# Reordering the start and the end of a seven-product up-projection in three chained transformer blocks

## The chip, the cores and the metric

The kernel runs on one core of a Trainium2 chip. The metric is device time in microseconds (us) of one execution, as the median of several runs. One execution was also recorded by the hardware profiler; the rows below come from it.

## The reference

The input is one sequence of 1024 tokens with 1024 features. Three blocks follow one another: the first mixes by retention and a gated unit, the second by convolution and neighbourhood attention, the third by stick-breaking and sliding-window attention. The change concerns the feed-forward parts of blocks 1 and 3, with D_FF = 2816:

```python
# block 1
h = rmsnorm(x, ffn_norm_g[l])
up = causal_depthwise_conv(h @ w_up[l], conv_w[l], conv_b[l])
a, bgate = jnp.split(up, [D_FF], axis=-1)
x = x + (jax.nn.silu(a) * bgate) @ w_down[l]
# block 3
gate, up = jnp.split(h @ w_gate_up, 2, axis=-1)
ffn = (jax.nn.silu(gate) * up) @ w_down
h = layer_norm_3(ALPHA * h + ffn, ln2_g[l], ln2_b[l])
```

## The kernel before

Activations lie with features on the 128 partitions and tokens along the free axis, in two halves of 512 tokens. Each fp32 product is made of three matmuls on split operands, `hi` (a copy in the matmul type, on ACT) and `lo` (the remainder `src - hi`, on DVE or POOL; `split`): hi·hi, lo·hi and hi·lo.

An up-projection has 22 chunks of 128 gate and 128 up features. The first `lead` chunks (3 in block 1, 2 in block 3) are plain products, two by `first_quad` (tile `fq`, 4 weight tiles `whi`/`wlo` in each token half) and, in block 1, chunk 2 by `gemm_a`. While `first_quad` computes, the normalization of the second half is still being made (tiles `rs_s`, `r`, `row`, `hhi`). The other chunks go through `strassen` (L1258): the 2 x 2 block product of (gate, up) weights and (feature, token) halves of the input, by seven products of 12 matmuls each, summed in three PSUM banks `p1`, `p2`, `p3`. Per group (one chunk, index `n`) the weights need sums and splits, in six steps `s0` to `s5` (`s_steps`, L1204): A22 (`shi`/`slo`); two sums on POOL (`raw<-raw`); S1 and S3 (`shi`/`slo`); A1 (`whi`/`wlo`); two more sums; S24 (`whi`/`wlo`). Steps of group n+1 are issued between the products of group n. The weights come in pairs of tiles `raw` by `s_dma`, from the buffer pools `wp` and `up` in turn. The input side needs T1 to T4, made once per block in `gen_t` (L1176): differences of `X` in place on DVE, then `thi` on ACT and `tlo`.

Of the sums, `e1` (copy of the first bank, on ACT) and `v1`, `v2` (bank plus `e1`, on DVE) lead to outputs; S3·T3 overwrites the bank that `v1` reads, A22·T4 the bank that `v2` reads. The outputs of a chunk go through convolution and silu (block 1: copy `u` by `put`, then `conv`: `carry`, `t`, `a`, `g`) or gating (block 3); `later(c)` returns this work as closures, which run during the next group. `g` goes to DRAM (`gd`) and comes back as `gx` for the down-projection.

The down-projection `down` (tile `dn`) takes the chunks in pairs: for each of 16 outputs six matmuls and one addition to `X`. Its preparation is `tail(0)` to `tail(3)`, issued between the products of the last group: weights, loads of `gx` and `X`, and the splits `ghi`/`glo`.

Nothing reorders the program: each engine runs its instructions in the order in which the code issues them, and waits at the first that is not ready. Banks of PSUM (6, tag `b`), `h` buffers (64) and the tiles `whi`, `wlo` (4 each) set how far one engine may run ahead.

Of the kernel before, what the change touches and what calls it, by code (L numbers as in the profile page):

```python
# [12 lines left out]
ALU = mybir.AluOpType  # L13
# [82 lines left out]

S_TILES = ((38, 76), (178, 218))

_VEC = [
    ("mix_norm_g", 8), ("ret_norm_g", 4), ("ffn_norm_g", 8), ("conv_b", 44), ("final_norm_g", 8),
# [196 lines left out]
class Kernel:  # L299
    def __init__(self, tc, ins, outs, blocks=(1, 2, 3)):  # L300
        self.tc, self.nc, self.a, self.o = tc, tc.nc, ins, outs
        self.blocks = blocks
        self.drv = Driver()
        self.wn = 0
        self.wl, self.raws = [], []
        self.wi = self.wd = 0
        self.stops = [lo for lo, _ in S_TILES]


    def h(self, name="h", dt=F32, shape=(128, HF), tag="h"):  # L310
# [45 lines left out]


    def w_dma(self):
        if self.wd < self.a["wall"].shape[0]:
            raw = self.wp.tile([128, 1024], F32, tag="raw", bufs=2, name="raw")  # L360
            self.nc.sync.dma_start(out=raw, in_=self.a["wall"][self.wd])
            self.wd += 1
            self.raws.append(raw)

    def w_more(self):
        return self.wi < (self.stops[0] if self.stops else self.a["wall"].shape[0])

    def w_load(self):

        if not self.w_more():  # L370
            return
        nc = self.nc
        while len(self.raws) < min(2, self.a["wall"].shape[0] - self.wi):
# [170 lines left out]
            self.drv.drain()  # L544


    def first_quad(self, evac, hook=None):

        ws = self.w_take(4)
        for half in range(2):
            self.drv.force(self.hs[half])
            pend = []
            for g in (0, 2):
                pss = [self.bank("fq") for _ in range(2)]
                if half == 1 and hook:
                    hook()
                yield from self.gemm_q(pss, ws[g:g + 2], half, middle=hook if half == 1 and g else None)
                pend += [(g + i, half, ps) for i, ps in enumerate(pss)]  # L560
                if half == 1:
# [614 lines left out]
    def gen_t(self):  # L1176

        X, T = self.X, self.T  # L1180
        V, P = self.nc.vector, self.nc.gpsimd

        def make(i, parts):

            low = None
            for k, (x, p, q) in enumerate(parts):
                hi, lo = T[i][0][k], T[i][1][k] = self.h("thi", F32R), self.h("tlo", F32R)
                self.tt(x, p, q, ALU.subtract)
                self.act(hi, x, AF.Copy)
                if low:  # L1190
                    self.tt(*low, ALU.subtract, V)
                low = lo, x, hi
            self.tt(*low, ALU.subtract, P)

        make(1, [(X[k][0], X[k][1], X[k][0]) for k in range(4)])
        yield
        make(2, [(X[k][0], X[k + 4][1], X[k][0]) for k in range(4)])
        yield
        make(3, [(X[k][1], X[k + 4][1], X[k][1]) for k in range(4)])
        yield  # L1200
        make(4, [(X[k + 4][0], X[k + 4][0], X[k][0]) for k in range(4)])
        yield

    def s_steps(self, n, st):  # L1204
# [16 lines left out]

        def s0():
            nonlocal ra, rb
            ra, rb = self.raws[0:2]
            self.raws = self.raws[2:]
            self.wi += 2
            st["A22"] = quarter(rb[:, R])

        def s1():
# [18 lines left out]

    def s_dma(self, n):

        pool = self.up if n % 2 else self.wp
        for _ in range(2):
            raw = pool.tile([128, 1024], F32, tag="raw", bufs=2, name="raw")
            self.nc.sync.dma_start(out=raw, in_=self.a["wall"][self.wd])
            self.wd += 1
            self.raws.append(raw)

    def strassen(self, lead, put, later, rest, tail):  # L1258

        hhi, hlo = self.H
        B11, B21, B22 = (([hhi[k + o][x] for k in range(4)], [hlo[k + o][x] for k in range(4)])
                         for o, x in ((0, 0), (4, 0), (4, 1)))
# [10 lines left out]
                    yield 6 * 216.0  # L1275

        n_all = NFF - lead
        left = ([], [], [])
        cur = self.s_first
        for n in range(n_all):  # L1280
            c = n + lead
            nxt, steps = {}, []
            b1, b2, b3 = (self.bank(x) for x in ("p1", "p2", "p3"))
            if n + 2 < n_all:
                self.s_dma(n + 2)
# [3 lines left out]
                steps[1]()  # L1289
            else:  # L1290
                tail(0)
                steps = [None] * 2 + [lambda: tail(1), lambda: None, lambda: tail(2), lambda: tail(3)]
            if n == 0:
                yield from prod(b1, cur["A1"], 0, B11, True)
                steps[2]()
                yield from prod(b3, cur["S1"], 0, T[1], True)
                yield from prod(b2, cur["S24"], 0, T[2], True)
            else:
                yield from prod(b2, cur["S24"], 0, T[2], True)
                steps[2]()  # L1300
                yield from prod(b1, cur["A1"], 0, B11, True)
            e1, v1 = self.h("e1"), self.h("v1")
            self.act(e1, b1, AF.Copy)
            self.tt(v1, b2, e1, ALU.add)
# [2 lines left out]
            steps[3]()  # L1307
            for f in left[0]:
                f()
            if n > 0:  # L1310
                yield from prod(b3, cur["S1"], 0, T[1], True)
            steps[4]()
            yield from prod(b2, cur["S3"], 0, T[3], False)
            v2 = self.h("v2")
            self.tt(v2, b2, e1, ALU.add)
            put(c, 1, 1, b3, v2)
            steps[5]()
            yield from prod(b1, cur["A1"], 512, B21, False)
# [8 lines left out]
            put(c, 0, 1, b3, v1)  # L1327
            left = later(c)
            cur = nxt
        for part in left:  # L1330
            for f in part:
                f()

    def ffn(self, evac, put, later, add_last, done, by_half, alpha=None, lead=2):

# [4 lines left out]
        with ExitStack() as ctx:  # L1340
            self.up = ctx.enter_context(self.tc.tile_pool(name="ffn", bufs=4))
            self.pt = ctx.enter_context(self.tc.tile_pool(name="ffnp", bufs=2, space=PSUM))
            self.T = {i: ([None] * 4, [None] * 4) for i in range(1, 5)}
            self.s_first = {}
            steps = self.s_steps(0, self.s_first)
            gt = self.gen_t()

            def step(n):
                for _ in range(n):
                    steps.pop(0)()  # L1350

            def hook():

                next(gt)
                if lead == 2:
                    step(2)
                    if len(steps) == 4:
# [6 lines left out]
            def g_split(c, half, own):  # L1364
# [3 lines left out]
                self.split(hi, lo, x, eng=nc.vector if half else None)  # L1368
                G[c, half] = hi, lo

            def g_group(i):
# [8 lines left out]
            def tail(n):  # L1380

                if n == 0:
                    del self.stops[0]
                    self.w_load()
                    self.w_load()
                elif n == 1:
                    for a in g_group(0):
                        g_dma(*a[:2])
                    for j in range(2):
                        x_load(j)  # L1390
                elif n == 2:
                    for a in g_group(0):
                        g_split(*a)
                else:
                    for j in range(2, 8):
                        x_load(j)
                    for a in g_group(1):
                        g_dma(*a[:2])

            yield from self.first_quad(lambda i, half, ps: evac(i // 2, i % 2, half, ps), hook)  # L1400
            for i in range(4, 2 * lead):
                w, = self.w_take(1)
                step(3)
                if i == 5:
                    self.s_dma(1)
                    next(gt)
# [6 lines left out]
            yield from self.strassen(lead, put, later, (lambda: next(gt)) if lead == 2 else (lambda: None), tail)  # L1413

            def down(i, ws):
                n = 0
# [2 lines left out]
                for j in range(8):  # L1419
                    for half in range(2):  # L1420
# [1034 lines left out]
```

## Time and profile before

| | us |
|---|---|
| median of 3 runs | 3191.98 |
| the runs | 3191.98, 3200.32, 3191.89 |
| the profiled execution | 3198.7 |
| its span | 3196.9 |
| PE busy | 2966.0 |

The span is what the trace shows from the first instruction to the last; 1.8 us of the profiled execution lie around it. Times in the rows are counted from the span's start. PE is TensorE's matmuls, PEld its weight loads, DVE VectorE, ACT ScalarE, POOL GpSimd, SP the engine that issues the DMAs. A number in brackets is the engine's idle time ahead of the instruction, with what ended it.

### The profile page before, as it was taken

Reading aid. Unit: us, or ns where it says so; the run is one execution under the profiler, and the core shown is the slowest. Engines: PE = TensorE matmul, PEld = TensorE weight load, DVE = VectorE, ACT = ScalarE, POOL = GpSimd, SP = SyncE. Lnnn points to the kernel's source line nnn. Section 1 sums busy time; section 2 is a strip of 40 time slices with the busy share of each in tenths; the row PEclk is TensorE's granted clock in tenths of the full one; section 3 lists DMA queues with packets and bytes.
Section 4 is the critical chain, followed back from the end, with each engine's and each line's share of the span. In section 5 each row is a group of like instructions: output and inputs, shape, how many; then the busy total and the mean of one; then the engine's idle time right before and its main releaser. Section 6 shows DMA issues by size and latency. Waiting matters only on the chain. (4 is left out here: it accounts for less than half of the span.)

```text
span 3196.9 us, 41418 instructions
## 1 busy us (share of the span) xinstructions
PE 2966.0 (93%) x15188; PEld 2512.3 (79%) x15188; DVE 1813.0 (57%) x3518; ACT 1287.2 (40%) x2493; POOL 1432.2 (45%) x1012
## 2 busy tenths in 40 slices
PE   8999996999989999889998989988799899999997
PEld 6898785888868878768897778877678688887886
DVE  6443255566665568976655664666767522224556
ACT  4232234444431243556673356644434422222223
POOL 4313424777733364863214352143333577674330
PEclk9999998999999999999998999989889999999997
DMA  4101231222243212131113232100212222225321
GB/s 156 34 21 54 73 115 52 77 80 80 79 158 106 94 52 86 37 96 58 46 38 116 92 121 63 45 19 22 67 66 96 83 79 80 88 74 175 102 83 53
DMA packets 114876, 248.96 MB, mean 78 GB/s; under 512 B 19696, under 2 KB 31600, under 8 KB 114672
## 3 DMA queue, kind: packets, MB, share of 16 engines
q1 hardware_dynamic: 114384, 246.01, 23.6%
q8 instruction: 120, 1.97, 0.3%
q14 instruction: 84, 0.69, 0.1%
q10 hardware_dynamic: 288, 0.30, 0.0%
HBM read 192.52 MB, written 53.74 MB: 77 GB/s over the span
## 5 line engine op out<-in xcount | busy, mean ns | idle before, releaser
L331 POOL TENSOR_TENSOR wlo<-raw,whi 128x1024 fp32r<-128x1024 f32 x240 | 581.4, 2432 | 868.2 <-ACT whi L325 827.4
L325 ACT ACTIVATE whi<-raw 128x1024 fp32r<-128x1024 f32 x240 | 248.0, 1053 | 566.8 <-PE dn L346 315.0
L331 DVE TENSOR_TENSOR X<-dn,X 128x512 f32<-128x512 f32 (+1 forms) x312 | 210.6, 677 | 173.4 <-PE dn L346 170.8
L346 PE MATMUL dn<-ghi,whi 128*128 128x512 f32 (+1 forms) x736 | 283.4, 385 | 5.9 <-DVE X L331 5.9
L346 PE MATMUL dn<-glo,whi 128*128 128x512 f32 (+1 forms) x736 | 282.6, 384 | 0.0
L346 PE MATMUL dn<-ghi,wlo 128*128 128x512 f32 (+1 forms) x736 | 282.3, 383 | 0.0
L346 PE MATMUL p<-thi,shi 128*128 128x512 f32 x468 | 187.8, 401 | 23.6 <-DVE v L331 22.8
L331 POOL TENSOR_TENSOR raw<-raw 128x512 f32<-128x512 f32 x156 | 201.9, 1295 | 12.1
L346 PE MATMUL p<-hhi,whi 128*128 128x512 f32 x468 | 184.5, 394 | 19.8 <-ACT whi L325 19.8
L331 DVE TENSOR_TENSOR v<-p,e 128x512 f32<-128x512 f32 x78 | 53.8, 690 | 247.8 <-ACT e L325 194.9
L346 PE MATMUL p<-hhi,wlo 128*128 128x512 f32 x468 | 184.3, 394 | 6.3 <-POOL wlo L331 6.3
L346 PE MATMUL p<-tlo,shi 128*128 128x512 f32 x468 | 186.1, 398 | 0.0
L331 POOL TENSOR_TENSOR slo<-raw,shi 128x512 fp32r<-128x512 f32 x117 | 150.7, 1302 | 78.6 <-ACT shi L325 78.6
L346 PE MATMUL p<-thi,slo 128*128 128x512 f32 x468 | 185.6, 397 | 0.0
L346 PE MATMUL p<-hlo,whi 128*128 128x512 f32 x468 | 183.4, 392 | 0.0
L328 DVE SCALAR_TENSOR_TENSOR t<-u,vec,t 128x512 f32<-128x512 f32 x176 | 133.0, 756 | 79.5 <-ACT t L325 74.1
L346 PE MATMUL qk<-hhi,whi 128*128 128x512 f32 x384 | 164.2, 428 | 8.0 <-ACT hhi L325 7.2
L331 POOL TENSOR_TENSOR beta<-beta,f 128x511 f32<-128x511 f32 (+3 forms) x96 | 89.3, 934 | 176.5 <-DVE beta L335 165.4
L346 PEld LDWEIGHTS dn<-ghi,whi 128*128 128x128 f32 x736 | 140.0, 190 | 34.1 <-DVE X L331 6.3
L346 PEld LDWEIGHTS dn<-glo,whi 128*128 128x128 f32 x736 | 140.1, 190 | 27.6
L346 PEld LDWEIGHTS dn<-ghi,wlo 128*128 128x128 f32 x736 | 140.0, 190 | 27.4
L346 PE MATMUL op<-hhi,wlo 128*128 128x512 f32 x384 | 153.5, 400 | 4.0 <-POOL wlo L331 4.0
(401 smaller groups left out, 8177.2 us busy)
## 6 DMA issues: line engine op xcount, KB each, us to landing
raw<-in_wall SPq DMA_DIRECT2D x240, 512.0 KB, 3.7
gd<-g SPq DMA_DIRECT2D x88, 256.0 KB, 2.1
gx<-gd SPq DMA_DIRECT2D x88, 256.0 KB, 4.9
x2d<-X SPq DMA_DIRECT2D x64, 256.0 KB, 2.0
X<-x2d SPq DMA_DIRECT2D x64, 256.0 KB, 5.4
x<-in_xT SPq DMA_DIRECT2D x16, 256.0 KB, 6.1
X<-in_xT SPq DMA_DIRECT2D x16, 256.0 KB, 4.4
T<-in_rpbx SPq DMA_DIRECT2D x8, 448.0 KB, 3.9
```

Source lines behind the costliest of these rows:

```text
L325: self.nc.scalar.activation(out=out, in_=in_, func=func, bias=bias, scale=scale, **kw)
L328: self.nc.vector.scalar_tensor_tensor(out=out, in0=in0, scalar=s, in1=in1, op0=op0, op1=op1)
L331: (eng or self.nc.vector).tensor_tensor(out=out, in0=in0, in1=in1, op=op)
L346: self.nc.tensor.matmul(out=out, lhsT=lhsT, rhs=rhs, start=start, stop=stop, skip_group_check=more)
```

## The change

The change alters the order of instructions, and for some the engine; the products, sums and loads are the same in number.

1. The first group's weights have a list of their own (`sraws`). In block 1 its pair of `raw` tiles is loaded at the start of `first_quad`, and s0 to s2 are issued in its first half (`hook` 1 to 3); s3 to s5 stand ahead of chunk 2. In block 3, s0 to s2 are issued in the first half, s3 to s5 in the second.
2. The input sums are made in the order T1, T3, T2, T4, all `tlo` on DVE; before, the fourth of each was on POOL.
3. The first group computes A1·B11, S24·T2, S1·T1; before, S1·T1 came second.
4. Chunk 2 of block 1 computes its second token half first, only copies its outputs (`put`), and leaves the convolutions to the first group (`later(2)`).
5. In the last group the loads of `gx` are issued behind the second product, and the splits of the first down-projection group behind `v2` and the first output, all four `glo` on POOL; before, they stood ahead of `v2`, two of them on DVE.
6. What is left of the last chunk is dealt out over the outputs of `down`; before, it stood ahead of them.

```diff
-S_TILES = ((38, 76), (178, 218))
+S_TILES = ((38, 38), (178, 180))
...
     def w_dma(self):
-        if self.wd < self.a["wall"].shape[0]:
+        if self.wd < self.stops[0][1]:
...
     def w_more(self):
-        return self.wi < (self.stops[0] if self.stops else self.a["wall"].shape[0])
+        return self.wi < self.stops[0][0]
...
     def first_quad(self, evac, hook=lambda n: None):
...
             for g in (0, 2):
                 pss = [self.bank("fq") for _ in range(2)]
-                if half == 1 and hook:
-                    hook()
-                yield from self.gemm_q(pss, ws[g:g + 2], half, middle=hook if half == 1 and g else None)
+                hook(4 * half + g)
+                yield from self.gemm_q(pss, ws[g:g + 2], half, middle=lambda: hook(4 * half + g + 1))
...
     def gen_t(self):
...
                 if low:
-                    self.tt(*low, ALU.subtract, V)
+                    self.tt(*low, ALU.subtract)
                 low = lo, x, hi
-            self.tt(*low, ALU.subtract, P)
+            self.tt(*low, ALU.subtract)
 
         make(1, [(X[k][0], X[k][1], X[k][0]) for k in range(4)])
         yield
+        make(3, [(X[k][1], X[k + 4][1], X[k][1]) for k in range(4)])
+        yield
         make(2, [(X[k][0], X[k + 4][1], X[k][0]) for k in range(4)])
-        yield
-        make(3, [(X[k][1], X[k + 4][1], X[k][1]) for k in range(4)])
         yield
         make(4, [(X[k + 4][0], X[k + 4][0], X[k][0]) for k in range(4)])
...
     def s_dma(self, n):
-        pool = self.up if n % 2 else self.wp
+        pool = self.up if (n + self.lead) % 2 else self.wp
...
     def strassen(self, put, left, later, rest, tail):
...
-        left = ([], [], [])
...
-                steps = [None] * 2 + [lambda: tail(1), lambda: None, lambda: tail(2), lambda: tail(3)]
-            if n == 0:
-                yield from prod(b1, cur["A1"], 0, B11, True)
-                steps[2]()
-                yield from prod(b3, cur["S1"], 0, T[1], True)
-                yield from prod(b2, cur["S24"], 0, T[2], True)
-            else:
+            if n > 0:
                 yield from prod(b2, cur["S24"], 0, T[2], True)
                 steps[2]()
-                yield from prod(b1, cur["A1"], 0, B11, True)
+            yield from prod(b1, cur["A1"], 0, B11, True)
+            if n == 0:
+                steps[2]()
+                yield from prod(b2, cur["S24"], 0, T[2], True)
+            if n + 1 == n_all:
+                tail(1)
...
-            if n > 0:
-                yield from prod(b3, cur["S1"], 0, T[1], True)
+            yield from prod(b3, cur["S1"], 0, T[1], True)
             steps[4]()
             yield from prod(b2, cur["S3"], 0, T[3], False)
             v2 = self.h("v2")
             self.tt(v2, b2, e1, ALU.add)
             put(c, 1, 1, b3, v2)
             steps[5]()
+            if n + 1 == n_all:
+                tail(2)
             yield from prod(b1, cur["A1"], 512, B21, False)
             put(c, 0, 0, b1, None)
             for f in left[1]:
                 f()
+            if n + 1 == n_all:
+                tail(3)
             yield from prod(b2, cur["A22"], 0, T[4], False)
...
-        for part in left:
-            for f in part:
-                f()
+        self.left = [f for part in left for f in part]
...
             def hook(n):
 
+                if n == 0 and lead == 3:
+                    self.s_dma(0)
+                elif n in (1, 2, 3):
                     steps.pop(0)()
+                elif n in (4, 6):
+                    next(gt)
+                    if n == 6 and lead == 2:
+                        for f in steps:
+                            f()
                         self.s_dma(1)
+                elif n == 7 and lead == 2:
+                    next(gt)
...
             def tail(n):
...
                 elif n == 2:
+                    for j in range(2, 5):
+                        x_load(j)
+                else:
                     for a in g_group(0):
-                        g_split(*a)
-                else:
-                    for j in range(2, 8):
+                        g_split(*a, nc.gpsimd)
+                    for j in range(5, 8):
                         x_load(j)
                     for a in g_group(1):
                         g_dma(*a[:2])
...
-            for i in range(4, 2 * lead):
-                w, = self.w_take(1)
-                step(3)
-                if i == 5:
-                    self.s_dma(1)
-                    next(gt)
-                for half in range(2):
-                    ps = self.bank("fq")
-                    yield from self.gemm_a(ps, w, half)
+            left = ([], [], [])
+            if lead == 3:
+                ws = self.w_take(2)
+                for f in steps:
+                    f()
+                self.s_dma(1)
+                for half in (1, 0):
+                    for w in range(2):
+                        ps = self.bank("fq")
+                        yield from self.gemm_a(ps, ws[w], half)
+                        put(2, w, half, ps, None)
                     if half:
-                        self.w_retire(1)
-                    evac(i // 2, i % 2, half, ps)
+                        next(gt)
+                        next(gt)
+                self.w_retire(2)
+                left = later(2)
...
             def down(i, ws):
...
                         n += 1
+                        if n % 3 == 1 and self.left:
+                            self.left.pop(0)()
                         if n % gap == 0 and loads and n > 2:
                             g_split(*loads.pop(0))
```

Three places in the instruction order. First, ACT at the end of the plain products of block 1 and in the first group of seven products (`u`, `t`, `a` are convolution work, `e` the copy `e1`). Before:

```order
149 L325 ACTIVATE u<-fq 128x512
150 L325 ACTIVATE t<-u,vec 128x512
151 L325 ACTIVATE shi<-raw 128x512 x3
152 L325 ACTIVATE u<-fq 128x512
153 L325 ACTIVATE t<-u,vec 128x512
154 L325 ACTIVATE a<-t 128x512
155 L325 ACTIVATE u<-fq 128x512
156 L325 ACTIVATE t<-u,vec 128x512
157 L325 ACTIVATE a<-t 128x512
158 L325 ACTIVATE whi<-raw 128x1024 x2
```

Now:

```order
152 L326 ACTIVATE u<-fq 128x512
153 L326 ACTIVATE t<-u,vec 128x512
154 L326 ACTIVATE whi<-raw 128x1024 x2
155 L326 ACTIVATE u<-fq 128x512 x2
156 L326 ACTIVATE thi<-X 128x512 x8
157 L326 ACTIVATE u<-fq 128x512 x2
158 L326 ACTIVATE shi<-raw 128x512 x3
159 L326 ACTIVATE e_4396<-p_4351 128x512
160 L326 ACTIVATE whi<-raw 128x1024
161 L326 ACTIVATE t<-u,vec 128x512
162 L326 ACTIVATE a<-t 128x512
163 L326 ACTIVATE t<-u,vec 128x512
```

The two `whi` copies (A1 and S24) move ahead of the convolutions of chunk 2; the three `shi` still stand ahead of `e`, and `thi` of T2 and T4 come behind `whi`.

Second, ACT in the first half of the plain products of block 1, ahead of the normalization of the second token half, where `rs_s` is the root that the rows `r` are made of. Before:

```order
122 L325 ACTIVATE whi<-raw 128x1024
123 L325 ACTIVATE sq<-X 128x512
124 L325 ACTIVATE rs_s<-ms 128x4
125 L325 ACTIVATE hhi<-X 128x512 x2
126 L325 ACTIVATE u<-fq 128x512
127 L325 ACTIVATE t<-u,vec 128x512
```

Now:

```order
122 L326 ACTIVATE whi<-raw 128x1024
123 L326 ACTIVATE sq<-X 128x512
124 L326 ACTIVATE shi<-raw 128x512
125 L326 ACTIVATE rs_s<-ms 128x4
126 L326 ACTIVATE hhi<-X 128x512 x2
127 L326 ACTIVATE u<-fq 128x512
128 L326 ACTIVATE t<-u,vec 128x512
```

One `shi`, of A22, stands ahead of `rs_s`.

Third, DVE in the last group of block 1. Before:

```order
707 L1109 COPY u<-carry 128x2
708 L328 SCALAR_TENSOR_TENSOR t<-u,vec,t 128x512 x2
709 L331 TENSOR_TENSOR glo<-gx,ghi 128x512 x2
710 L331 TENSOR_TENSOR v_7400<-p_7282,e_7340 128x512
711 L331 TENSOR_TENSOR u<-p_7283,v_7400 128x512
```

Now:

```order
707 L1109 COPY u<-carry 128x2
708 L329 SCALAR_TENSOR_TENSOR t<-u,vec,t 128x512 x2
709 L332 TENSOR_TENSOR v_7384<-p_7282,e_7340 128x512
710 L332 TENSOR_TENSOR u<-p_7283,v_7384 128x512
711 L1105 MEMSET u 128x2
712 L1107 COPY carry<-u 128x2
```

The two `glo` are gone from the row ahead of the second sum `v`.

## Rows read from the trace of the kernel before

**Rows 1.** Page, section 1: busy time, share of the span and instructions of each engine.

```profile
PE 2966.0 (93%) x15188; PEld 2512.3 (79%) x15188; DVE 1813.0 (57%) x3518; ACT 1287.2 (40%) x2493; POOL 1432.2 (45%) x1012
```

**Rows 2.** Waits of PE, whole span: us in total, times, longest us.

```profile
PE p L346 <- DVE v L331: 22.8, 4, 8.7
PE p L346 <- ACT whi L325: 21.0, 3, 16.9
...
PE p L346 <- POOL wlo L331: 9.7, 4, 5.1
...
PE dn L346 <- DVE X L331: 5.9, 1, 5.9
```

**Rows 3.** Windows: us, busy time (instructions) of each engine, granted clock of PE, DMA share, GB/s.

```profile
557.47:575.00 17.53, 17.53 (x65) 14.21 (x66) 2.77 (x4) 3.55 (x6) 14.15 (x10) 0.84 0.36 112
575.00:900.00 325.00, 325.00 (x1414) 265.68 (x1414) 203.89 (x355) 148.25 (x218) 227.96 (x148) 1.00 0.22 76
921.14:928.45 7.31, 7.30 (x24) 5.87 (x25) 5.33 (x11) 0.78 (x1) 0.00 (x0) 0.75 1.05 387
942.69:960.00 17.31, 17.31 (x64) 14.04 (x65) 10.82 (x17) 1.41 (x2) 2.00 (x3) 0.83 0.40 136
...
2909.97:2917.80 7.83, 7.83 (x25) 6.24 (x25) 2.07 (x3) 0.00 (x0) 0.00 (x0) 0.69 1.05 396
```

**Rows 4.** Timeline, all engines, 455 to 465: start us, us, engine, line, operation, tiles [idle before].

```profile
460.21 0.20 ACT L325 ACTIVATE rs_s<-ms 128x4 f32<-128x4 f32 x1 [2.87 <-DVE ms L335]
...
461.26 0.16 DVE L331 TENSOR_TENSOR r<-rs_s,rs_t 128x4 f32<-128x4 f32 x1
...
464.27 0.60 PE L454 MATMUL row<-ident,r 128*128 128x128 f32 x4
```

**Rows 5.** Page, section 6: DMA issues, KB each, median us from issue to landing.

```profile
raw<-in_wall SPq DMA_DIRECT2D x240, 512.0 KB, 3.7
```

**Rows 6.** Page, section 5: groups of POOL and ACT instructions, busy us, mean ns of one, idle before.

```profile
L331 POOL TENSOR_TENSOR wlo<-raw,whi 128x1024 fp32r<-128x1024 f32 x240 | 581.4, 2432 | 868.2 <-ACT whi L325 827.4
L325 ACT ACTIVATE whi<-raw 128x1024 fp32r<-128x1024 f32 x240 | 248.0, 1053 | 566.8 <-PE dn L346 315.0
...
L331 POOL TENSOR_TENSOR raw<-raw 128x512 f32<-128x512 f32 x156 | 201.9, 1295 | 12.1
```

**Rows 7.** Timeline, all engines, 536 to 558.

```profile
536.59 0.79 PE L346 MATMUL p<-hhi,whi 128*128 128x512 f32 x1 [16.93 <-ACT whi L325]
...
542.85 2.41 POOL L331 TENSOR_TENSOR wlo<-raw,whi 128x1024 fp32r<-128x1024 f32 x1 [1.17 <-ACT whi L325]
...
543.33 2.48 DVE L331 TENSOR_TENSOR tlo<-X,thi 128x512 fp32r<-128x512 f32 x1 [7.23 <-ACT thi L325]
...
550.84 0.61 ACT L325 ACTIVATE shi<-raw 128x512 fp32r<-128x512 f32 x1
...
557.47 0.79 PE L346 MATMUL p<-thi,shi 128*128 128x512 f32 x1 [8.71 <-DVE v L331]
```

**Rows 8.** Timeline, all engines, 918 to 922.

```profile
918.67 1.26 POOL L331 TENSOR_TENSOR glo<-gx,ghi 128x512 fp32r<-128x512 f32 x1 [0.68 <-ACT ghi L325]
...
920.41 0.68 DVE L331 TENSOR_TENSOR v<-p,e 128x512 f32<-128x512 f32 x1
...
921.14 0.79 PE L346 MATMUL p<-thi,shi 128*128 128x512 f32 x1 [6.47 <-DVE v L331]
```

**Rows 9.** Waits of PE, window 2440 to 2562.

```profile
PE p L346 <- POOL wlo L331: 8.5, 3, 5.1
PE p L346 <- ACT whi L325: 4.1, 2, 2.8
PE p L346 <- DVE v L331: 2.0, 1, 2.0
```

**Rows 10.** Timeline, all engines, 2906 to 2910.

```profile
2906.61 1.30 ACT L325 ACTIVATE ghi<-gx 128x512 fp32r<-128x512 f32 x2 [0.25 <-DMA gx<-gd]
...
2909.97 0.80 PE L346 MATMUL p<-thi,shi 128*128 128x512 f32 x1 [5.59 <-DVE v L331]
```

More of the change, by code (lines that the diff above doesn't have):

```diff
@@ L304, in __init__ @@
         self.wn = 0
-        self.wl, self.raws = [], []
+        self.wl, self.raws, self.sraws = [], [], []
         self.wi = self.wd = 0
-        self.stops = [lo for lo, _ in S_TILES]
+        n = self.a["wall"].shape[0]
+        self.stops = [*S_TILES, (n, n)]
     def h(self, name="h", dt=F32, shape=(128, HF), tag="h"):
@@ L372, in w_load @@
         nc = self.nc
-        while len(self.raws) < min(2, self.a["wall"].shape[0] - self.wi):
+        while len(self.raws) < min(2, self.stops[0][1] - self.wi):
             self.w_dma()
@@ L544, in build, with first_quad @@
             self.drv.drain()
-    def first_quad(self, evac, hook=None):
+    def first_quad(self, evac, hook=lambda n: None):
         ws = self.w_take(4)
@@ L1180, in gen_t @@
         X, T = self.X, self.T
-        V, P = self.nc.vector, self.nc.gpsimd
         def make(i, parts):
@@ L1223, in s0 @@
             nonlocal ra, rb
-            ra, rb = self.raws[0:2]
-            self.raws = self.raws[2:]
-            self.wi += 2
+            raws = self.sraws or self.raws
+            ra, rb = raws.pop(0), raws.pop(0)
             st["A22"] = quarter(rb[:, R])
@@ L1255, in s_dma, with strassen @@
             self.wd += 1
-            self.raws.append(raw)
-    def strassen(self, lead, put, later, rest, tail):
+            self.sraws.append(raw)
+    def strassen(self, put, left, later, rest, tail):
+        lead = self.lead
         hhi, hlo = self.H
@@ L1281, in strassen @@
             c = n + lead
-            nxt, steps = {}, []
+            nxt, steps = {}, [lambda: None] * 6
             b1, b2, b3 = (self.bank(x) for x in ("p1", "p2", "p3"))
@@ L1343, in ffn, with hook @@
             self.T = {i: ([None] * 4, [None] * 4) for i in range(1, 5)}
-            self.s_first = {}
+            self.s_first, self.lead = {}, lead
             steps = self.s_steps(0, self.s_first)
             gt = self.gen_t()
-            def step(n):
-                for _ in range(n):
+            def hook(n):
+                if n == 0 and lead == 3:
+                    self.s_dma(0)
+                elif n in (1, 2, 3):
                     steps.pop(0)()
-            def hook():
-                next(gt)
-                if lead == 2:
-                    step(2)
-                    if len(steps) == 4:
+                elif n in (4, 6):
[3 more added lines that the diff above has]
+                            f()
                         self.s_dma(1)
+                elif n == 7 and lead == 2:
+                    next(gt)
             def g_dma(c, half):
@@ L1362, in g_dma, with g_split @@
                 nc.sync.dma_start(out=G[c, half], in_=self.gd[c][:, HF * half:HF * half + HF])
-            def g_split(c, half, own):
+            def g_split(c, half, own, eng=None):
                 x = G[c, half]
@@ L1367, in g_split @@
                           for y in ("ghi", "glo"))
-                self.split(hi, lo, x, eng=nc.vector if half else None)
+                self.split(hi, lo, x, eng=eng or (nc.vector if half else None))
                 G[c, half] = hi, lo
@@ L1383, in tail @@
                     del self.stops[0]
+                    self.wi += 2 * (NFF - lead)
                     self.w_load()
@@ L1400, in ffn @@
             yield from self.first_quad(lambda i, half, ps: evac(i // 2, i % 2, half, ps), hook)
-            for i in range(4, 2 * lead):
-                w, = self.w_take(1)
-                step(3)
-                if i == 5:
-                    self.s_dma(1)
-                    next(gt)
-                for half in range(2):
-                    ps = self.bank("fq")
-                    yield from self.gemm_a(ps, w, half)
-                    if half:
-                        self.w_retire(1)
-                    evac(i // 2, i % 2, half, ps)
-            yield from self.strassen(lead, put, later, (lambda: next(gt)) if lead == 2 else (lambda: None), tail)
+            left = ([], [], [])
[9 more added lines that the diff above has]
+                        put(2, w, half, ps, None)
+                    if half:
+                        next(gt)
+                        next(gt)
+                self.w_retire(2)
+                left = later(2)
+            yield from self.strassen(put, left, later, (lambda: next(gt)) if lead == 2 else (lambda: None), tail)
             def down(i, ws):
```

## The prediction

> **What bounds the kernel now.** I read the page first: TensorE (PE) is busy for 2966.0 of 3196.9 us [rows 1], so time can only come out of the 231 us in which it idles, and out of stretches in which it runs slowly. Next I read the list of what PE waited for over the whole program [rows 2], where the reader should look at tile names: waits of `p`, the seven-product scheme, are 22.8 us on the sum `v`, 21.0 on the weight copy `whi` and 9.7 on the weight remainder `wlo`; `dn`, the down-projection, has one wait of 5.9 on `X`. The change touches only tiles of these kinds. A timeline of PE then shows where they lie: at the first group and behind the last group of products in blocks 1 and 3. I call the four places A (start, block 1), B (end, block 1), C (start, block 3) and D (end, block 3).
>
> A wait costs more than its length. In the steady part of block 1, 1414 matmuls take 325.0 us at granted clock 1.00, which is 0.230 us each. Behind the wait that ends at 557.47, 65 take 17.53 us at 0.84, instead of 14.9; behind 921.14, 24 take 7.30 instead of 5.5; behind 942.69, 64 take 17.31 instead of 14.7; behind 2909.97, 25 take 7.83 instead of 5.8 [rows 3]. So 1.8 to 2.6 us come on top of each longer wait. Granted clocks of 0.69 to 0.84 over a window are mixtures of the two levels, 2.4 and 1.2 GHz.
>
> **Place A.** Chunk 2's plain products end at 519.66 (536.59 less 16.93), and the fourth seven-product matmul group, S3·T3, starts at 557.47 [rows 7]. That is 37.8 us for 36 matmuls, which at 0.230 are worth 8.3; 29.5 us are lost. Two waits make most of it: 16.93, because ACT does the convolutions of chunk 2 ahead of `whi`, and 8.71, because ACT does three `shi` that wait for sums on POOL ahead of the copy `e` that `v` needs.
>
> Now the same stretch with the new order. The first pair of weights is loaded early, and its first `shi` stands on ACT ahead of `rs_s`, the root for the normalization. In the trace `rs_s` ran at 460.21, its result `r` was there at 461.42, and PE used it at 464.27 [rows 4]. A weight tile lands 3.7 us after its issue in the median [rows 5]; two tiles behind the copies that SP issues there I put at 465.8. Then `shi` ends at 466.4, `r` is ready 1.2 later, at 467.6, and PE stands still 3.4 us. Another 0.5 goes to the remainders of chunk 2, whose place on POOL moves back. Chunk 2 ends at 519.66 + 3.9 = 523.6.
>
> Because chunk 2's convolutions are now left for the next group, ACT copies A1's `whi` before that end; I put its end at 518.4. POOL follows with `wlo` (2.43), two sums (1.30 each) and, after one `whi` copy of 1.05, the next `wlo` [rows 6]: 520.9, 523.5, 524.6, 527.0. A1·B11 waits for nothing. S24·T2 needs the last `wlo` and four T2 remainders on DVE, which alternate with differences behind the POOL instruction: 530.3. S24·T2 ends near 531, S1·T1 near 533.7. Behind T4's four copies ACT starts the three `shi` of the next group at about 536.0, and from the first `shi` to S3·T3 it took 6.63 before (550.84 to 557.47 [rows 7]) with the same instructions in between. So S3·T3 starts at 542.6, 14.9 us sooner. Bounds: if the early tiles land at once, 18; if they land 7 us later than I think, 8. The 8.7 wait is not cured, it stays at 8.9: `e` still stands behind `shi`. **14.9.**
>
> **Place B.** PE waits 6.47 for `v` at 921.14; DVE did that sum at 920.41, behind two remainders `glo`, which wait for `gx` from memory [rows 8]. With all four `glo` on POOL and behind the second sum, `v` follows the last convolution directly, and I put its end at 916.1; as PE was free at 914.67, 1.5 of the wait is left. Gain 5.0, and 1.8 of slow matmuls behind it. Four `glo` at 1.26 on POOL [rows 8] end at about 923.2 if the first starts at 918.0; the down-projection, now due at 921.6, needs its third then, and the fourth for its second output. That just fits. The 5.9 us on `X` [rows 2] came because all left-over convolutions stood ahead of the first `X` on DVE; dealt out over the down-projection they fit into the six banks that PE may fill ahead, worth some 8 us, of which I see 2.6 used. Gain 5.9, and 2.6 behind it. Bounds: 5 to 18. **15.3.**
>
> **Place C.** Waits of 8.5, 4.1 and 2.0 in the window [rows 9]. Weights come earlier (two steps in the first half) and T1, T3 are formed before T2, so that S1·T1 and S3·T3 are ready when wanted. What is late next is T2: its copies stand behind the `whi` of S24, which I put at 2512.4, and its last remainder at 2518.0. By the same chain as in A, S3·T3 starts at 2524.5, which is 6.0 before its place in the trace; I take 5.5, since PE will again be slow behind the 4.8 us wait that is left. Bounds: 0 to 11. **5.5.**
>
> **Place D.** PE waits 5.59 at 2909.97 for `v` behind `glo` again, and the last two of the copies `ghi` that they follow come at 2906.61 to 2907.91 [rows 10]. Now `v` is ready before PE is, about 0.3 of the wait stays, and 2.1 of slow matmuls goes: 7.4. The four `glo` on POOL follow the copies and end at 2909.7 and 2910.9 for the third and fourth, when the down-projection comes to them at 2909.7: no slack at all. Bounds: 0 to 7.7. **7.4.**
>
> The rest costs nothing that I see. All fourth T remainders go from POOL to DVE (eight in all), an 0.68 instruction instead of 1.3, in stretches where DVE waits anyway. The loads of `X` for the down-projection move back by up to 3 us on SP, ahead of need. The pair of `raw` buffers changes pools, and no buffer is wanted before it was freed.
>
> The sum is 14.9 + 15.3 + 5.5 + 7.4 = 43.1 us. The profiled execution took 3198.7 us (its span and 1.8 us around it), so 3155.6 for that one; it stands 6.7 above the median of the runs, 3192.0, from which 43.1 leaves 3148.9. I forecast 3149.
>
> **Rivals.** First, *the starts trade one wait for another* (3161). In A and C the T2 remainders come on DVE while POOL works on weights. At 543.33 such a remainder took 2.48 where 0.68 is what a DVE sum takes: POOL had begun a `wlo` at 542.85, which ended at 545.26, and the DVE instruction ended 0.55 after that [rows 7, 8]. If four of them in C each met a POOL instruction of 1.3, T2 would come 5 us later and C would gain nothing; the same in A, and a slower landing, would take A to 8. Gain 8 + 15.3 + 0 + 7.4 = 31. Against it: POOL's next work in A waits for ACT. The Trainium skill says of this (SBUF — State Buffer, "Who interferes with whom") that a VectorE instruction with two SBUF inputs and a GpSimd instruction that reads SBUF exclude each other for a whole instruction, whereas one SBUF input does not contend. The row of 2.48 agrees with that; taken strictly for every T remainder, the rule gives this rival's time and not mine.
>
> Second, *the remainders on POOL hold up the down-projection* (3159). At B and D the third and fourth `glo` have no slack. If `gx` lands 2 us later than before, or if POOL gets behind, PE waits 3 us at each place and is slow for 2 behind it: 10 less, 33. For it: at D the copies follow the landing directly [rows 10]. Against it: the loads are issued where they were.
>
> Third, *slower than before*: ACT takes its instructions in order, so `shi` ahead of `rs_s` ties the whole first half of block 1's up-projection to one load. Each microsecond that the pair lands after about 462.4 (464.27 less 1.2 and 0.6) costs PE one. I count 3.4 of that already. To eat up the 43 us and go over by 10, the pair would have to land near 515, 56 us after its issue, where the median is 3.7 [rows 4, 5]. Only a full DMA queue, or a buffer of the other pool that is not free until then, would do it; I saw neither.
>
> Fourth, *nothing changes*: what is saved in the four places is waited for later, for instance on weight loads. Against it, in the 325 us behind A PE does not wait at all [rows 3], so the loads keep up there with slack.
>
> **How the numbers follow.** Forecast 0.61; starts trade waits 0.20; remainders on POOL 0.12; no change 0.04; slower 0.03. A measurement of this kernel tells 0.3% from no change, 9.6 us. The first three cases are faster by 31 to 43, together 0.93. The range: the lower bounds of all four places at once (8, 5, 0, 0) would be a gain of 13, the upper ones (18, 18, 11, 7.7) one of 55; the first two rivals together give 43.1 − 12.1 − 10 = 21. Since the bounds won't all be met at once, I take a gain of 18 to 55, 3137 to 3174, which leaves out the last two cases and the far ends of the others, 2 in 10.
>
> **What would show it.** Right: no wait of `p` on `whi` near 520 to 537 and one of about 9 on `v` near 534; a new wait of about 3 of PE on the tile `row` near 465; at B no wait of `dn` on `X`, and one of under 2 on `v`; at D none over 1; at C three or four waits, none over 5. Wrong: `row` waiting over 10; `dn` waiting for `glo`; S24·T2 waiting for `tlo` in A over 5; a steady part of either up-projection with new waits.

## The result and the profile after

The changed kernel takes 3151.31 us (median of 4 runs, 3148.27 to 3154.91), the kernel before 3194.38 in the same comparison. The ratio is 0.9863, with a 95% interval of 0.9844 to 0.9882: 43.1 us less. 3149 was forecast. The total came out, but one step of the sum was mis-sized by 5 us, and a term of 5 to 7 us that no step had is in it. One run of the variant `e_first` below was slow, at 8262.43 us, and is left out there.

Section 1 of the changed kernel's page, which answers to [rows 1], for a span of 3153.1 us:

```profile
PE 2957.1 (94%) x15188; PEld 2514.3 (80%) x15188; DVE 1808.9 (57%) x3522; ACT 1286.6 (41%) x2493; POOL 1429.0 (45%) x1008
```

The waits of PE (us in total, times, longest) in three windows of the changed kernel, 440 to 575 (place A), 890 to 960 (B) and 2400 to 2530 (C); at D there is none:

```profile
PE p L347 <- DVE u L1105: 8.4, 1, 8.4
PE row L455 <- DVE r L332: 5.2, 1, 5.2
PE fq L347 <- POOL wlo L332: 1.6, 2, 1.1
PE p L347 <- DVE tlo L332: 1.5, 3, 1.0
...
PE p L347 <- DVE v L332: 1.4, 1, 1.4
...
PE dn L347 <- DVE X L332: 0.6, 1, 0.6
...
PE p L347 <- POOL wlo L332: 3.4, 2, 1.7
PE p L347 <- ACT thi L326: 2.1, 1, 2.1
PE p L347 <- DVE tlo L332: 2.0, 1, 2.0
PE p L347 <- DVE v L332: 1.9, 2, 1.2
```

Against [rows 2, 9]: the 16.9 on `whi` is gone, the 5.9 on `X` has become 0.6, and those on `v` at B and D are 1.4 and nothing. At C no wait is over 2.1. A wait of 5.2 on `row` is new. The 8.7 of place A is still there, with 8.4 (put down to `u`, but the `v` that DVE did just before is what PE needs).

To find where the time went, look up one instruction in both traces and subtract; between two such rows lies what the stretch gained:

| instruction (start, us) | before | after | difference | stretch ahead of it |
|---|---|---|---|---|
| `rs_s`, first normalization of block 1 | 429.23 | 425.00 | 4.2 | same program |
| end of chunk 2 (first `p`, less its wait) | 519.66 | 523.91 | -4.2 | A, first part: -8.5 |
| first matmul of S3·T3 | 557.47 | 543.44 | 14.0 | A, second part: +18.3 |
| `e`, block 1's last group | 907.49 | 888.56 | 18.9 | 18 groups: +4.9 |
| 49th `dn` of block 1 (its ninth output) | 947.98 | 913.54 | 34.4 | B: +15.5 |
| `rs_s` behind block 1 | 1195.10 | 1158.82 | 36.3 | rest of `down`: +1.8 |
| `rs_s`, last one ahead of C | 2476.39 | 2448.56 | 27.8 | same program: -8.5 |
| `e`, second group of block 3 | 2552.57 | 2517.71 | 34.9 | C: +7.0 |
| first `dn` of block 3 | 2917.80 | 2874.80 | 43.0 | D: +8.1 |

The four places give 9.8 + 15.5 + 7.0 + 8.1 = 40.4. Stretches of the same program vary between executions: from its first `dn` to the first product of C the changed kernel took 1576.1 us, the variant `order_s1_second` below, with the same program there, 1571.9. So nothing is read out of +4.2 and -8.5. The +4.9 over groups whose work is the same is another matter.

### The profile page after: what moved, and what is told of

It is laid out like the page before. It is cut to its first block, busy times and chain, and to the rows that moved or that the text cites. A ratio compares the mean times of both kernels' runs of the same rounds, so it can differ in the third digit from the quotient of the medians.

```text
span 3153.1 us, 41402 instructions
## 1 busy us (share of the span) xinstructions
PE 2957.1 (94%) x15188; PEld 2514.3 (80%) x15188; DVE 1808.9 (57%) x3522; ACT 1286.6 (41%) x2493; POOL 1429.0 (45%) x1008
## 5 line engine op out<-in xcount | busy, mean ns | idle before, releaser
L347 PE MATMUL qk<-hlo,whi 128*128 128x512 f32 x384 | 156.3, 407 | 1.5 <-DVE hlo L329 1.5
```

The lines of the kernel that those rows point to most:

```text
L347: self.nc.tensor.matmul(out=out, lhsT=lhsT, rhs=rhs, start=start, stop=stop, skip_group_check=more)
```

## The experiments

**The kernel before, once more** (no edit).

> The kernel before, profiled a second time; nothing is changed. In its first profile a group of seven products took 19.32 us in block 1 (19.04 in the changed kernel) and 19.10 in block 3, which adds up to 4.9 us over block 1's groups and some 2 in its down-projection, in code that the change leaves alone; and the unchanged start of the program was 4.2 us longer, while parts of blocks 2 and 3 were 8.4 shorter. Theory: this is difference between two executions. Then the period of block 1 falls to about 19.05 here, or the offsets have other sizes. Rival: it belongs to the program (where its buffers lie). Then the period is 19.32 again and the offsets come back to within 0.5 us.

The group's period in block 1 is 19.32 us again, while the first `rs_s` comes at 426.88 instead of 429.23. So the offsets are differences between executions, and the slower step belongs to the program: the theory held for the first and fell for the second.

**The ends alone** (the kernel before with `tail`, `g_split`, `down` and the places of `tail(1)` to `tail(3)` as the diff of the change has them) and **the starts alone** (the changed kernel with the lines of these as they were).

> The kernel before with the change's parts 5 and 6 alone (loads and splits of the last group behind its sums, on POOL; left-overs dealt out in the down-projection). Theory: the two ends are worth 15.5 us (B) and 8.0 us (D) and do not depend on the starts: 23.5 us less than before, ratio 0.9926, and the waits of 16.9 and 8.7 in A and the six of C stay. Rival: the ends gain only because the loads come at another time relative to the weights of the changed start; then under 12 us, ratio above 0.996.

> The changed kernel with the ends of the kernel before (parts 1 to 4 alone). Theory: A is worth 9.8 us and C 7.0 us: 17 us less than before, ratio 0.9947, with the waits of 6.5 on v and 5.9 on X of place B and 5.6 of place D back. Rival: starts and ends depend on each other; then the two parts' gains add up to less than 35 or more than 46 us.

The ends give 3173.71 us, ratio 0.9933 (0.9918 to 0.9948), about 21 us; the starts 3173.30, ratio 0.9937 (0.9918 to 0.9955), about 20. The 23.5 and 17 that were expected lie in these intervals. Added, 41 of the 43: nothing says that the halves depend on each other, though intervals of 5 to 6 us either way would hide a small dependence. The traces say the same by place: with the ends alone the waits of 16.9 and 8.6 in A stay, with the starts alone 6.8 on `v` and 5.9 on `X` at B and 5.3 on `v` at D are back. The group's period is 19.32 with the ends alone and 19.04 with the starts alone, so the faster step comes with the starts.

**The first weight steps later** in block 1:

```diff
-                elif n in (1, 2, 3):
+                elif n in ((3, 4, 5) if lead == 3 else (1, 2, 3)):
                     steps.pop(0)()
-                elif n in (4, 6):
+                if n in (4, 6):
...
```

> The changed kernel, but in block 1 the three first weight steps of the first group are issued in the second token half of the plain products (hooks 3, 4, 5 for 1, 2, 3); the loads stay where they are. Theory: the 5.2 us wait of PE on the tile row, the slow matmuls behind it and the waits on fq weights behind it are the price of shi standing ahead of rs_s on ACT, 8.3 us in all to the end of chunk 2. They go, nothing else in A comes later, and S3*T3 starts 6 to 8 us sooner. Rival: PE waits there for the loads that share the DMA queues with the pair, and the row wait stays at 3 us or more. Second rival: the steps now collide with T1 and T3 on DVE, and what is gained on row is lost at S24*T2 (a wait on tlo or wlo of over 3 us).

Waits of PE in `shi_late`, 440 to 575:

```profile
...
PE fq L347 <- POOL wlo L332: 3.2, 2, 2.7
...
```

The wait on `row` is gone, and from the first `rs_s` to `e` it takes 110.2 us instead of 117.1: 6.9 less, as expected. But the waits on the `fq` weights did not go, they grew from 1.6 to 3.2, and the end of chunk 2, 94.5 us behind the first `rs_s`, lies between the kernel before (90.4) and the changed one (98.9). To the first `dn` only 2.3 of the 6.9 are left (475.4 against 477.7): the period is 19.32. One execution, 3150.79 us, can't be told from the changed kernel.

**`e1` first** in block 1's first group, and the same with the later weight steps:

```diff
             if n == 0:
-                steps[2]()
+                if lead == 2:
+                    steps[2]()
                 yield from prod(b2, cur["S24"], 0, T[2], True)
...
             if n == 0:
+                if lead == 3:
+                    steps[2]()
                 rest()
...
                     if half:
                         next(gt)
-                        next(gt)
...
```

(`rest` then makes T4 in block 1 too.)

> The changed kernel, but in block 1's first group the copy e1 and the sum v1 stand ahead of the two later shi of the next group, and T4 is made behind them. Theory: the 8.4 us wait of place A is e1 queued on ACT behind three shi (which wait for POOL) and T4's copies. It shrinks to 1 us or less, S3*T3 starts 7 to 8 us sooner; 1 to 3 us of it come back as waits on whi or wlo at the second group, whose weights then start later on POOL. Net 5 to 7 us less than the changed kernel. Rival: POOL's chain for the second group (about 14 us from its first shi to its last wlo) is the real bound; then the second group waits 6 us or more and the net is under 2. Second question: a group of seven products took 19.32 us in block 1 in the kernel before and in shi_late, 19.04 in the changed kernel and in starts_only. If the wait on the tile row ahead of the products goes with the faster level, it is 19.04 here, where that wait stays.

> shi_late and e_first together. Theory: both are local, so S3*T3 starts 12 to 14 us sooner than in the changed kernel. By the observation of shi_late the period of a group in block 1 goes to 19.32, which takes 6 to 7 us back by the end of the down-projection; net 5 to 9 less than the changed kernel. Rival: the period is 19.04, then 12 to 14.

`e_first`: 3145.90 us (median of three runs), ratio 0.9852 (0.9829 to 0.9875). `e` comes 10.0 us sooner after `rs_s`, the wait of 8.4 is gone, and all of it comes back: to the first `dn` it takes 478.0 us, against 477.7. Of the 5 to 7 us that were expected none is left; the rival's net of under 2 came, but neither theory nor rival named the place. It is A22·T4, which waits for `v2`, which stands on DVE behind two convolutions of chunk 2. The timeline of `e_first`, DVE and PE (the row puts the wait down to `a`, but PE starts right behind `v`):

```profile
547.56 1.55 DVE L329 SCALAR_TENSOR_TENSOR t<-u,vec,t 128x512 f32<-128x512 f32 x2 [0.84 <-ACT t L326]
...
550.50 1.54 DVE L329 SCALAR_TENSOR_TENSOR t<-u,vec,t 128x512 f32<-128x512 f32 x2 [1.20 <-ACT t L326]
551.96 0.68 DVE L332 TENSOR_TENSOR v<-p,e 128x512 f32<-128x512 f32 x1
...
552.79 0.77 PE L347 MATMUL p<-thi,shi 128*128 128x512 f32 x1 [8.96 <-ACT a L326]
```

The period is 19.04 in `e_first` (with a wait of 5.1 on `row`) and 19.32 in `late_e_first` (none), which took 3144.74 us, ratio 0.9854 (0.9838 to 0.9869). Neither ratio can be told from the changed kernel's 0.9863. Of the 5 to 9 us expected of `late_e_first`, 1.2 are there at the first `dn` (476.5 us behind `rs_s`): it too waits 8.9 us at A22·T4.

**Order or engine at the ends**, and **the left-overs**: the splits back at their old place but all on POOL; and the left-overs ahead of `down`.

```diff
             steps[4]()
+            if n + 1 == n_all:
+                tail(4)
             yield from prod(b2, cur["S3"], 0, T[3], False)
...
-                else:
+                elif n == 4:
                     for a in g_group(0):
                         g_split(*a, nc.gpsimd)
+                else:
...
```

```diff
-        self.left = [f for part in left for f in part]
+        self.left = []
+        for part in left:
+            for f in part:
+                f()
```

> The changed kernel with the splits of the first down-projection group at their old place, ahead of v2, but all four remainders on POOL. It tells order from engine. Theory: v2 was late because two remainders stood ahead of it on DVE; with none of them on DVE it is on time, so the wait of PE on v in B and D stays at 1.5 and 0; ACT now waits for gx in front of the copies of the first output, which costs under 2 us as that bank is wanted only by the down-projection. Rival: the order is what counts, since ACT's wait for gx holds up the convolutions whose sums DVE does ahead of v2; then the wait on v is back at 4 us or more in B.

> The changed kernel with the left-overs of the last chunk ahead of the down-projection again. Theory: place B gets back the wait of 5.9 us on X and the slow matmuls behind it, 8.5 us in all up to the third pair of outputs; D changes by less than 1, as block 3 has one short left-over. Rival: the wait went because the down-projection starts 7 us sooner and DVE's queue has other work by then; then the wait is under 3 us.

Waits of PE at B (875 to 975), first `splits_pool_early`:

```profile
PE p L347 <- DVE v L332: 1.5, 1, 1.5
...
```

then `no_spread`:

```profile
PE dn L347 <- DVE X L332: 6.4, 1, 6.4
...
```

At D there is no wait in either. So at B and D the engine of the remainders is what counts, not their place behind the sums, and the wait on `X` is the left-overs' alone. Both expectations held; one execution of each (3152.79 and 3151.07 us) says no more.

**Chunk 2 as before** and **S1·T1 second**:

```diff
-                for half in (1, 0):
+                for half in (0, 1):
...
-                        put(2, w, half, ps, None)
+                        evac(2, w, half, ps)
...
-                left = later(2)
```

```diff
                 steps[2]()
+                yield from prod(b3, cur["S1"], 0, T[1], True)
                 yield from prod(b2, cur["S24"], 0, T[2], True)
...
-            yield from prod(b3, cur["S1"], 0, T[1], True)
+            if n > 0:
+                yield from prod(b3, cur["S1"], 0, T[1], True)
```

> The changed kernel with part 4 undone: chunk 2 of block 1 in the old order of token halves, with its convolutions as its outputs come. Theory: the 16.9 us wait of the kernel before came from these convolutions ahead of whi on ACT; with whi now issued ahead of chunk 2 (part 1) it does not come back, but the convolutions stand ahead of T2's and T4's copies on ACT and of their differences on DVE, so that T2 is 5 to 8 us later, and S24*T2 waits that long. Rival: part 4 is what removed the wait; then one of over 12 us is back at the first products. Second rival: it does not matter (under 2 us), since the convolutions are only done earlier and the first group has less to do.

> The changed kernel with part 3 undone: S1*T1 second and S24*T2 third in the first group. Theory: S1 and T1 are ready early, S24 and T2 late; with S1*T1 second PE has 2.7 us of ready work while S24's remainder and T2's are made, so the waits on tlo in A (1.5) go and C's waits ahead of S24*T2 (1.7, 2.1, 2.0) shrink by 2 to 3, while the wait on v grows by as much, because v needs S24*T2. Net within 1 us in A, and in C within 1. So part 3 is worth nothing by itself. Rival: S24's bank is needed early for v1, and S3*T3 comes 2.7 us later in both places.

Waits of PE with the old chunk 2 (`chunk2_plain`), 440 to 575:

```profile
PE p L347 <- ACT thi L326: 13.4, 1, 13.4
PE p L347 <- DVE v L332: 6.8, 1, 6.8
...
```

S24·T2 waits the 13.4 us for `thi`, S3·T3 the 6.8 for `v`; it starts at 555.20 instead of 543.44. The place was the theory's, the size the rival's (over 12), 11.8 later instead of 5 to 8: the wait of 16.9 turns from one on `whi` into one on T2. That is more than the 9.8 that A gains, so without part 4 nothing of it is left. The edit undoes both halves of part 4, the order of the token halves and the postponed convolutions; which of them counts is not told apart. With S1·T1 second, the waits of 1.5 on `tlo` are gone, the one ahead of S3·T3 is 11.1 instead of 8.4, and S3·T3 starts at 543.26; in C it starts 18.9 us behind the first product in both kernels. Part 3 is worth nothing by itself, as expected.

**Where the operands lie.** One thing was found in the compiled programs that follows the two periods (their addresses are in no trace). In the pool `up` the buffers of a tag lie in the order in which the tags are first used. Where the convolutions' `u` (514 columns) comes first, the twelve buffers of tag `e` (`shi`, `slo`, some `ghi`, `glo`) lie at 416 modulo 2048 bytes in block 1; where `shi` comes first, at 288, as all other matmul operands do. The early weight steps of part 1 put `shi` first. The test, on the kernel before:

```diff
...
+        pair = [self.up.tile([128, 512], F32R, tag="e", bufs=12, name=x) for x in ("shi", "slo")] if n == 0 else None
...
-            st["A22"] = quarter(rb[:, R])
+            st["A22"] = quarter(rb[:, R], pair)
```

> The kernel before, with the first two tiles of the tag e (shi and slo of the first group) allocated at the start of the feed-forward part, so that their buffers lie ahead of those of u in the pool. Nothing else changes, no instruction moves. Observation so far: the kernels with 19.32 us a group in block 1 (before, ends_only, shi_late, late_e_first) have the buffers of tag e (shi, slo, ghi, glo) 128 bytes off all other matmul operands, modulo 2048; those with 19.04 (the changed kernel, starts_only, e_first, no_spread, splits_pool_early) don't, since there shi is allocated before u. In the kernel before, S and A22 products step by 0.231 to 0.234 us a matmul, S24 products by 0.227. Theory: the place of these buffers sets the step. Then the period is 19.04 here, block 1's down-projection steps by 0.227, and the kernel is 6 to 7 us faster than before, ratio 0.998. Rival: the wait on the tile row, which all kernels of the faster level have and none of the slower, sets it. Then nothing changes.

The window 575 to 880, busy time and count of instructions of PE, PEld, DVE, ACT, POOL, then the granted clock. The kernel before, second profile:

```profile
575.00:880.00 305.00, 305.00 (x1328) 249.36 (x1327) 193.28 (x335) 140.78 (x208) 218.80 (x143) 1.00 0.23 79
```

`before_placed`:

```profile
575.00:880.00 305.00, 305.00 (x1347) 252.55 (x1346) 194.22 (x336) 140.90 (x209) 220.47 (x144) 1.00 0.23 80
```

the changed kernel:

```profile
575.00:880.00 305.00, 305.00 (x1347) 252.71 (x1346) 194.47 (x338) 139.97 (x207) 218.68 (x143) 1.00 0.23 80
```

`shi_late`:

```profile
575.00:880.00 305.00, 305.00 (x1327) 249.35 (x1326) 192.14 (x334) 139.49 (x205) 214.39 (x139) 1.00 0.22 79
```

PE is busy throughout at the same granted clock, and does 1347 matmuls instead of 1328. With the place of the buffers alone the kernel before takes 3188.91 us, ratio 0.9978 (0.9968 to 0.9988), 7 us less, and the period is 19.04. The theory holds, the rival (the wait on `row`) falls: `before_placed` has no such wait. The run moves the buffers of `u` as well, but the products tell which move counts. In this window of the kernel before, matmuls that read `shi` or `slo` take 232 to 234 ns in the mean from start to start, those that read `whi` or `wlo` 226 to 229; in `before_placed` all take 226 to 227. In the down-projection, which reads `ghi` and `glo`, the step goes from 230 to 227 ns (960 to 1125).

**A version from these findings**: later weight steps, early `pair`, `e1` and T4 ahead of the second group's S1 and S3, and in the first group

```diff
             self.tt(v2, b2, e1, ALU.add)
+            if n == 0:
+                for f in left[0]:
+                    f()
             put(c, 1, 1, b3, v2)
```

with `left[0]` not done ahead of S1·T1 there.

> The changed kernel with what the runs point to, in block 1: the three first weight steps in the second token half (no wait on row), tag e allocated early (faster step), e1 and T4 ahead of the two later shi of the second group, and chunk 2's first convolutions behind v2 in the first group. Theory: against the changed kernel 8 us from the row wait (shi_late had taken 7 to the start of the products), up to 8 from the wait in A, of which late_e_first got nothing back because A22*T4 then waited 9.0 us for v2 behind the convolutions; here some 5 of it stay. 11 to 14 us less than the changed kernel, 3136 to 3140, ratio to before 0.982. Rival: the second group's weights come as late as ever (POOL), and the net is the row wait alone, 7 to 8 us less, 3143.

It takes 3134.33 us, ratio to before 0.9814 (0.9795 to 0.9833): about 16 us less than the changed kernel's 0.9863 of the same 3195, a little past the theory's best. Place A has waits of 1.1 and 3.3 on sums and 3.2 on `fq` weights left, none on `row`; from the first `rs_s` to the first `dn` it takes 466.6 us instead of 477.7, and the period is 19.04.

## Why the prediction was right, and where not

**A was 5 us too high**, 9.8 instead of 14.9, and the step that failed is the price of the early weight steps up to the end of chunk 2, "3.4 us" for `shi` ahead of `rs_s` and "another 0.5" for chunk 2's remainders on POOL: it came to 8.5, of which 5.7 stand at the first `fq` matmul behind `row` and 2.7 come after it. The timeline of the changed kernel, all engines, 462 to 466:

```profile
462.67 0.63 ACT L326 ACTIVATE shi<-raw 128x512 fp32r<-128x512 f32 x1 [9.54 <-DMA raw<-in_wall]
463.20 0.19 ACT L326 ACTIVATE rs_s<-ms 128x4 f32<-128x4 f32 x1
463.37 1.26 POOL L332 TENSOR_TENSOR slo<-raw,shi 128x512 fp32r<-128x512 f32 x1 [9.27 <-ACT shi L326]
...
463.63 1.02 DVE L332 TENSOR_TENSOR rs_t<-rs_s 128x4 f32<-128x4 f32 x1
...
465.08 0.16 DVE L332 TENSOR_TENSOR r<-rs_s,rs_t 128x4 f32<-128x4 f32 x1
```

ACT waits 9.5 us for the load; counted from the first `rs_s`, `shi` starts 1.1 us later than I put it. Then comes a thing I had left out: POOL starts `slo` right behind `shi`, and DVE's small product `rs_t` takes 1.02 us, until `slo` is done, where it took 0.16 in the trace of before (timeline, 455 to 465):

```profile
460.66 0.16 DVE L331 TENSOR_TENSOR rs_t<-rs_s 128x4 f32<-128x4 f32 x1
```

PE waits 5.2, goes on slowly (granted clock 0.50, the 1.2 GHz level, in the window 465 to 470), and waits 1.1 more for `wlo` of its weights than before. The prediction had put 1.8 to 2.6 us on top of each longer wait, but nothing on top of this one. That the 0.5 was too low whatever `shi` does is shown by `shi_late`: there `rs_s` is on time, and chunk 2 still ends 4.1 us later than before. The second part of A was right within a microsecond: 19.5 us from the end of chunk 2 to S3·T3, 19.0 predicted, with the wait that I said would stay: `shi` at 536.87 (536.0), `e` at 542.09.

**B was right in each term**: 6.9 at the first sum and the slow matmuls (5.0 + 1.8), 8.6 at `X` (5.9 + 2.6). That the four `glo` on POOL just fit held as well: `dn` doesn't wait for them. **C** gave 7.0 instead of 5.5, inside its bounds; no run takes C apart, so its cause is read from the waits alone. **D** gave 8.1 instead of 7.4, a little above its bound of 7.7. Of the signs, that C would have three or four waits was off: there are six, none over 2.1.

**The rivals.** The starts do trade waits (8.4 stays, 5.2 is new), and in A the gain of 9.8 is nearer to the first rival's 8 than to the 14.9. But its own cause, remainders of T2 beside POOL, is small: the waits on T2's copies and remainders are 1.5 us in A and 4.1 in C, and C gains 7.0 where the rival has nothing. The second didn't happen. The third has its mechanism shown, with a wait of 5.2 us instead of the 40 and more that would decide. The fourth fell: what was saved is not waited for later.

**What made up for A** is a term that I had answered with "costs nothing that I see": the order of first use in a pool. It is 4.9 us over the groups of block 1 and some 2 in its down-projection. The 0.230 us that the prediction took for a matmul at full clock held this already. With it the places add up to 47 us, inside the interval of the measured 43 (38 to 50). The forecast of 3149 was right within 3 us because an error of -5 and an omission of +5 to 7 met, which is luck.

## What to carry to other kernels

An instruction that waits for a load belongs behind whatever the same engine owes to the critical path, however early it could be issued: with the first `shi` ahead of `rs_s` PE waited 5.2 us on `row`, and with it and the two steps after it moved behind, the first group's fourth product came 6.8 us sooner. When a wait is removed, look for the instructions queued next on the same engine, as their wait can be of the same length (8.4 on `e`, then 9.0 on `v2`). And when an equal loop changes its period between two kernels, compare operand addresses too, and not only what happens in time.

## What the runs showed of the hardware

With the buffers of one operand tag elsewhere (by the compiled programs 128 bytes off the others modulo 2048), the step of dense matmuls was 0.230 us instead of 0.226 in the mean at the same granted clock, with a run for it (`before_placed`). That the offset modulo 2048 is what counts is not shown: which accesses collide is open, and other offsets were not tried. The 1.02 us of `rs_t` beside `slo` agrees with the rule of the Trainium skill cited ahead (SBUF — State Buffer, "Who interferes with whom"). What the rule says of one SBUF input holds there outside VectorE's 2-port modes, which the prediction left out. The price is what is left of the POOL instruction (`slo` ends at 464.63, `rs_t` at 464.65), so a 128x4 instruction of 0.16 us can take six times as long.
